# A hybrid attention and recurrence layer on one core: order around the last attention pair, and an engine for two copies

## The chip, the cores and the metric

The kernel runs on one core of one Trainium2 chip. The core has a matrix engine (TensorE, PE in the profile), VectorE (DVE), ScalarE (ACT), GpSimd (POOL), and queues that issue DMA transfers, of which SyncE's (SP) carries most. Each engine executes its own list of instructions in the order in which the program was built; engines wait for one another through semaphores. The metric is the device time of one execution in microseconds. Before the change three runs took 955.73 to 956.14 us, with a median of 955.91 us.

## The reference

One layer works on 1024 tokens of width 1024, with 16 learned tokens put in front (1040 columns in all):

```python
u = rmsnorm(h, g_pre_mix)
z = u @ w_in                      # -> q 512 | k 128 | v 128 | x_rec 512 | y_rec 512
attn = sliding_window_attention_with_sinks(q, k, v, sinks)   # window 128, 8 heads of 64, 2 kv heads
xr = causal_depthwise_conv(x_rec, conv_w, conv_b)            # 4 taps
hr = rg_lru(xr, w_a, b_a, w_x, b_x, lam)                     # two gates, then a linear scan over time
rec = gelu(y_rec) * hr
h = h + rmsnorm(concat(attn, rec) @ w_out, g_post_mix)
f = square(relu(rmsnorm(h, g_pre_ffn) @ w_ff1)) @ w_ff2      # 1024 -> 4096 -> 1024
out = h + rmsnorm(f, g_post_ffn)
```

Everything is float32. In the attention, each row of scores has its maximum taken (with the sink in it), then exp(s - m), the sum, the division, and the product with v.

## The kernel before, in words

Float32 accuracy is reached by splitting: every operand is held as a high part (rounded to the matrix engine's fast format, by a copy, L96 or L117) and a low part (the rest, by a subtraction on VectorE, L99 or L118). `mm3` (L123) makes a product of three matmuls: high with high (L125), high with low (L128), low with high (L129).

The work up to about 262 us is the mixing part, and it is what the change touches. After it come the output projection's rest and the feed-forward part, which take the remaining 690 us and which the diff does not touch.

The attention's eight query heads are treated as four pairs, j = 0 to 3. A pair is worked in two halves of 512 tokens, and a half in two steps bp of 256 tokens. `scores(j, half, q)` (L579) makes the score matmuls (L596, L600) into banks of PSUM with the tag "s", of which there are two; one bank holds one head's two blocks (i = 0, 1). VectorE takes each block's negated maximum (L616, one instruction that also writes the masked scores to SBUF and so empties that block), ScalarE the exponential (L624, seen as L82 in the profile, which is the line of the helper `lut`), GpSimd and VectorE sum and scale (L628 to L633). `attend(j, half, pairs)` (L637) transposes the result on the matrix engine (L644, banks "pt"), splits it (L96, L99), lets GpSimd cut the two sides of the window out of the two parts (L648, four of them in a step), and multiplies with v (L658: six matmuls in a step, banks "o"); ScalarE and VectorE then take the banks out (L671, L672).

Between the steps of the attention the kernel puts projections as fill for the matrix engine, one per half in the order q1, x1, q2, x2, q3, x3, y0, y1, then y2 and, behind the gates' code, y3. `project` (L257) runs each in pieces (two of 512 columns for q and y, four of 272 or 256 for x), with KC = 8 times `mm3` a piece, into banks "acc", of which there are two. Its `sink` takes the piece out of its bank:

- for q (L447), two 64-row halves, each a high part on ScalarE (L117) and then a low part on VectorE (L118);
- for x (L459), copies on ScalarE (L460);
- for y (L714), one copy on VectorE (L715). The y are the pieces that gate the recurrence.

A projection's weights are split when the one before it is begun (L96 and L99 into "ws", two pairs of buffers).

The recurrence is four chunks c. `gates(c)` (L789) multiplies the convolved x chunk with the gate weights (L800, into banks "s", "pt" and "o") and applies tanh; `decay`, `root`, `input_scale`, `input_gate`, `scan` and `rec_mult` follow, and with them the loads and splits of w_out (`load_wo`, L870; `split_wo`, L877). I call this the recurrent lane. Its VectorE order is written out by hand from L904 on with `queue`.

The order on each engine is made by a planner when the program is built: it takes, of the instructions that are ready by its own clock, the one with the smallest priority, which is the place in the program plus a delay of 1000 (FILL_LAG) for all of the fill but q1, q2 and q3 (`deferred`). Buffers of a tag go to whoever is planned to need one next. Three devices bend that order: `behind(name, ins)` (L106), which keeps `ins` behind the named instruction; `lut`, which chains all table functions on ScalarE; and `queue`. Two places use `behind` here: the low part of y0's weights stands behind the fourth maximum of pair 3 (L622), and the second piece of y1 is cut in two:

```python
if kc == 1 and begun is not None:            # L268, in project
    begun.append(ins)
if (c, t0) == (0, 696):                      # L806, in gates
    behind(ins.name, begun[1][1])
```

So `begun[1][1]` is the first matmul of kc = 1 in y1's second piece; it and what follows it in that piece stand behind the last gate matmul of chunk 0, and its three matmuls of kc = 0 may run ahead.

Of the kernel before, what the change touches and what calls it, by code (L numbers as in the profile page):

```python
# [18 lines left out]
KC = D // P  # L19
T = 1024  # L20
NMETA = 16
TT = T + NMETA
HD = 64
# [14 lines left out]
def hybrid_layer(  # L38
# [218 lines left out]
    def project(w, pieces, sink, begun=None):  # L257
        wh, wl = w
        for t0, n in pieces:
            acc = bank("acc")  # L260
            for kc in range(KC):
                uh, ul = u[kc]
                ins = mm3(
                    acc[:, :n], (wh[:, kc, :], wl[:, kc, :]),
                    (uh[:, t0 : t0 + n], ul[:, t0 : t0 + n]),
                    kc == 0, kc == KC - 1,
                )
                if kc == 1 and begun is not None:  # L268
                    begun.append(ins)
            sink(acc[:, :n], t0, n)  # L270

# [166 lines left out]
    def sink_v(acc, t0, n):  # L438
        if t0 == 0:
            nc.scalar.copy(vmt[:, META], acc[:, 0:NMETA])  # L440
        nc.scalar.copy(vt[:, t0 : t0 + n], acc)

    def new_q():

        q = pair("b", [P, T])

        def sink_q(acc, t0, n):  # L447
            c = slice(t0 - NMETA, t0 - NMETA + n)
            for h in range(2):
                r, o = HALF[h], HALF[1 - h]  # L450
                split_scaled(q[h][r, c], q[h][o, c], acc[r], HD ** -0.5)

        return q, sink_q

# [124 lines left out]
    def scores(j, half, q):  # L579

        g, pairs = j // 2, []
        for bp in range(2):
            sn = slot("c", [P, 4, 257])
            negm = small.tile([P, 4], F32, name="negm", tag="negm")
            den = small.tile([P, 4], F32, name="den", tag="den")
            rden = small.tile([P, 4], F32, name="rden", tag="rden")
            nc.vector.tensor_copy(
                sn.rearrange("p (h i) k -> p h i k", h=2)[:, :, :, 256],
                nsink[:, 2 * j : 2 * j + 2].to_broadcast([P, 2, 2]),
            )  # L590
            for h in range(2):
                sp_ = bank("s", (P, 2, 256))

                def qk(dst, b, hi, lo):
                    c = slice(b * P, (b + 1) * P)
                    nc.tensor.matmul(  # L596
                        dst, q[h][:, c], hi, start=True, stop=False,
                        skip_group_check=True,
                    )
                    nc.tensor.matmul(  # L600
                        dst, q[h][:, c], lo, start=False, stop=True,
                        skip_group_check=True,
                    )

                for i in range(2):
                    b = 4 * half + 2 * bp + i
                    if b == 0:
                        qk(sp_[:, i, 0:P], b, km[:, g, 0, :], km[:, g, 1, :])
                        qk(sp_[:, i, P:256], b, khh[g][:, 0:P], kl[g][:, 0:P])
                    else:  # L610
                        c = slice((b - 1) * P, (b + 1) * P)
                        qk(sp_[:, i, :], b, khh[g][:, c], kl[g][:, c])
                for i in range(2):
                    b = 4 * half + 2 * bp + i
                    k = 2 * h + i
                    top = nc.vector.tensor_tensor_reduce(  # L616
                        out=sn[:, k, 0:256], in0=sp_[:, i, :],
                        in1=mask1 if b == 0 else mask, scale=-1.0,
                        scalar=nsink[:, 2 * j + h : 2 * j + h + 1],
                        op0=ALU.add, op1=ALU.min, accum_out=negm[:, k : k + 1],  # L620
                    ).ins
                    if (j, half, bp, k) == (3, 0, 0, 3):  # L622
                        behind(top.name, *held_back)
                    lut(  # L624
                        sn[:, k, :], sn[:, k, :], AF.Exp, scale=-1.0,
                        bias=negm[:, k : k + 1], accum_out=den[:, k : k + 1],
                    )
            nc.vector.reciprocal(rden, den)  # L628


            one = sn[:, :, 0:P]
            nc.gpsimd.tensor_tensor(one, one, sn[:, :, P:256], op=ALU.add)
            nc.vector.tensor_tensor(one, one, rden.to_broadcast([P, 4, P]), op=ALU.mult)  # L633
            pairs.append(sn)
        return pairs

    def attend(j, half, pairs):  # L637
        g = j // 2
        o_ = slot("e", [P, 512])
        for bp, sn in enumerate(pairs):  # L640
            mh, ml = pair("c", [P, 4, 2, P])
            pt = bank("pt", (P, 4, P))
            for k in range(4):
                nc.tensor.transpose(pt[:, k, :], sn[:, k, 0:P], ident)  # L644
            split(mh[:, :, 1, :], ml[:, :, 1, :], pt)
            for m in (mh, ml):
                for side, op, sign in ((0, ALU.is_gt, 1), (1, ALU.is_ge, -1)):
                    nc.gpsimd.affine_select(  # L648
                        out=m[:, :, side, :], in_=f32(m)[:, :, 1, :],
                        pattern=[[0, 4], [-sign, P]], compare_op=op, fill=0.0,  # L650
                        base=0, channel_multiplier=sign,
                    )
            po = bank("o", (P, 2, 256))
            mhv, mlv = (m.rearrange("p (h i) s q -> p h (i s q)", h=2) for m in (mh, ml))

            def av(v, oc, n, pc, first, last):
                for k, m in enumerate((mhv, mlv)):
                    nc.tensor.matmul(  # L658
                        po[:, :, oc : oc + n], v, m[:, :, pc : pc + n],
                        start=first and k == 0, stop=last and k == 1,  # L660
                        skip_group_check=True,
                    )

            b = 4 * half + 2 * bp
            av(vk[g][:, b, :], 0, 256, P, True, False)
            av(vm[:, g, :] if b == 0 else vk[g][:, b - 1, :], 0, P, 0, False, False)
            av(vk[g][:, b + 1, :], P, P, 3 * P, False, True)
            c = slice(256 * bp, 256 * bp + 256)
            for h in range(2):
                r, o = HALF[h], HALF[1 - h]  # L670
                nc.scalar.copy(o_[r, c], po[o, h, :])  # L671
                nc.vector.tensor_tensor(o_[r, c], po[r, h, :], o_[r, c], op=ALU.add)  # L672
        ah, al = at[half][j // 2]
        split(ah[:, j % 2, :], al[:, j % 2, :], o_)
# [35 lines left out]
    def fill_y(c):  # L710
        def run(w):
            y = slot("b" if c == 1 else "d", [P, T])

            def sink(acc, t0, n):  # L714
                nc.vector.tensor_copy(y[:, t0 - NMETA : t0 - NMETA + n], acc)  # L715

            begun[c] = []
            project(w, REAL2, sink, begun[c])
# [70 lines left out]
    def gates(c):  # L789
# [3 lines left out]
        for t0, n in ((0, 348), (348, 348), (696, 344)):  # L793
# [10 lines left out]
                    if hold:  # L804
                        behind(hold, ins)
            if (c, t0) == (0, 696):  # L806
                behind(ins.name, begun[1][1])
            for s, t_ in enumerate((te, to)):
                shut[0] = lut(
                    t_[:, t0 : t0 + n], accs[s][:, :n], AF.Tanh, scale=0.5,  # L810
# [713 lines left out]
```

## Time and profile before

| | |
|---|---|
| median of three runs | 955.91 us (955.73 to 956.14) |
| the profiled execution | 955.25 us |
| its span, first to last instruction | 953.5 us |
| PE busy | 942.0 us, 99% of the span |
| DVE, ACT, POOL busy | 682.4, 498.3, 152.7 us |
| granted TensorE clock | 0.998 |

A row of a timeline has the start in us, the length in us, the engine, the line, the operation, the tiles written and read, the shape and the count of instructions merged into it; in brackets stands the idle time ahead of it and who ended it. A wait's row has the engine, tile and line that waited, the engine, tile and line that released it, and the total in us, the number of times and the longest. Matmuls overlap in the engine, so the distance from start to start is what one costs, not its length.

### The profile page before, as it was taken

The page shows a single profiled execution, that of the slowest core. Times are in us where ns is not written, and L with a number is a line of the kernel's source. Part 1 is how long each engine was busy: PE and PEld are TensorE (multiplying, and loading weights), DVE is VectorE, ACT ScalarE, POOL GpSimd, SP SyncE. Part 2 cuts the span into 40 slices and gives each one's busy share as a digit, 9 for nine tenths or more (in the row PEclk, how much of TensorE's full clock was granted, in tenths as well). Part 3 has the DMA queues.
Part 4 walks back from the last instruction along what each step waited for, and adds up shares of the span by engine and source line. Part 5 has one row for each costly group of instructions (what it writes and reads, how often), then busy time and mean ns, then how long its engine had stood idle before and what let it go on. Part 6 is the DMA issues. An engine that isn't in the chain of part 4 may idle for free.

```text
span 953.5 us, 12448 instructions
## 1 busy us (share of the span) xinstructions
PE 942.0 (99%) x4677; PEld 785.7 (82%) x4677; DVE 682.4 (72%) x968; ACT 498.3 (52%) x822; POOL 152.7 (16%) x196
## 2 busy tenths in 40 slices
PE   9999999999999999999999999999999999999997
PEld 8999998878788877888888878888888888888886
DVE  6679999777966886665755566567567676779884
ACT  7556676468355564443655565664433343445451
POOL 2115666500021100000111001100111100003020
PEclk9999999999999999999999999999999999999999
DMA  8121101203145457485646457644678865656422
GB/s 293 49 56 34 45 2 34 67 17 117 42 166 192 153 181 238 158 284 177 218 160 216 157 177 217 226 153 109 171 179 188 208 218 185 185 190 155 116 84 89
DMA packets 85629, 140.76 MB, mean 148 GB/s; under 512 B 5785, under 2 KB 48937, under 8 KB 85569
## 3 DMA queue, kind: packets, MB, share of 16 engines
q1 hardware_dynamic: 75104, 108.51, 36.1%
q0 software_dynamic: 9600, 29.36, 11.7%
q10 hardware_dynamic: 864, 2.10, 0.6%
q8 instruction: 37, 0.61, 0.3%
q14 instruction: 24, 0.19, 0.1%
HBM read 115.70 MB, written 23.07 MB: 146 GB/s over the span
## 4 chain that ended last, share of the span: by engine, by line
PE 88%; DVE 7%; ACT 2%; issue 1%; DMA 1%; POOL 1%; DVEq 0%; SPq 0%; ACTq 0%; POOLq 0%
PE ps_acc L125 10%; PE ps_acc L128 10%; PE ps_acc L129 10%; PE ps_pt L128 6%; PE ps_pt L129 6%; PE ps_pt L125 6%; PE ps_s L125 6%; PE ps_s L129 6%; PE ps_s L128 6%; PE ps_o L125 5%; PE ps_o L128 5%; PE ps_o L129 5%; DVE c L852 1%; PE ps_o L658 1%; PE ps_o L996 1%
## 5 line engine op out<-in xcount | busy, mean ns | idle before, releaser
L96 ACT CAST ws<-raw 128x1024 fp32r<-128x1024 f32 (+1 forms) x70 | 71.8, 1025 | 118.9 <-PE ps_o L128 45.8
L99 DVE TENSOR_TENSOR ws<-raw,ws 128x1024 fp32r<-128x1024 f32 (+1 forms) x71 | 85.4, 1203 | 45.5 <-ACT ws L96 45.5
L125 PE MATMUL ps_acc<-a,ws 128*128 128x256 f32 (+2 forms) x256 | 85.5, 334 | 1.1 <-ACT d L460 1.0
L129 PE MATMUL ps_acc<-a,ws 128*128 128x256 f32 (+2 forms) x256 | 85.0, 333 | 0.0
L128 PE MATMUL ps_acc<-a,ws 128*128 128x256 f32 (+2 forms) x256 | 85.0, 332 | 0.0
L99 DVE TENSOR_TENSOR b<-b,b 128x1024 fp32r<-128x1024 f32 (+2 forms) x48 | 57.6, 1199 | 25.5 <-PE ps_o L128 19.8
L96 ACT CAST ws<-e 128x1024 fp32r<-128x1024 f32 x42 | 44.0, 1047 | 57.0 <-PE ps_o L128 31.4
L96 ACT CAST b<-b 128x1024 fp32r<-128x1024 f32 (+2 forms) x48 | 49.5, 1030 | 38.8 <-DVE b L1022 36.4
L99 DVE TENSOR_TENSOR ws<-e,ws 128x1024 fp32r<-128x1024 f32 x42 | 51.3, 1222 | 20.0 <-ACT ws L96 20.0
L648 POOL TENSOR_SCALAR_AFFINE_SELECT c<-c 128x512 fp32r<-128x512 f32 x64 | 55.8, 893 | 26.8 <-ACT c L96 20.6
L125 PEld LDWEIGHTS ps_acc<-a,ws 128*128 128x128 f32 x256 | 48.2, 188 | 6.4 <-ACT d L460 1.2
L129 PEld LDWEIGHTS ps_acc<-a,ws 128*128 128x128 f32 x256 | 48.2, 188 | 5.1 <-issue 0.2
L178 POOL TENSOR_TENSOR rs<-ms,half_pow 128x1 f32<-128x1 f32 x26 | 19.3, 749 | 205.9 <-DVE ms L174 204.7
L128 PEld LDWEIGHTS ps_acc<-a,ws 128*128 128x128 f32 x256 | 48.1, 188 | 4.6 <-issue 0.4
L125 PE MATMUL ps_acc<-ws,b 128*128 128x512 f32 (+1 forms) x120 | 46.3, 385 | 0.0
L129 PE MATMUL ps_acc<-ws,b 128*128 128x512 f32 (+1 forms) x120 | 46.2, 385 | 0.0
L128 PE MATMUL ps_acc<-ws,b 128*128 128x512 f32 (+1 forms) x120 | 46.1, 384 | 0.0
L125 PE MATMUL ps_pt<-ws,b 128*128 128x512 f32 x112 | 44.2, 394 | 0.0
L128 PE MATMUL ps_pt<-ws,b 128*128 128x512 f32 x112 | 44.1, 393 | 0.0
L129 PE MATMUL ps_pt<-ws,b 128*128 128x512 f32 x112 | 43.9, 392 | 0.0
L125 PE MATMUL ps_s<-ws,b 128*128 128x512 f32 x110 | 43.4, 395 | 0.0
L129 PE MATMUL ps_s<-ws,b 128*128 128x512 f32 x110 | 43.2, 393 | 0.0
(429 smaller groups left out, 2720.9 us busy)
## 6 DMA issues: line engine op xcount, KB each, us to landing
raw<-in_w_ff_dram SPq DMA_DIRECT2D x58, 512.0 KB, 4.4
e<-in_w_ff_dram SPq DMA_DIRECT2D x42, 512.0 KB, 4.1
raw<-in_w_in_dram SPq DMA_DIRECT2D x12, 512.0 KB, 5.1
d<-in_w_ff_dram SPq DMA_DIRECT2D x12, 512.0 KB, 4.2
s_dram<-d POOLq DMA_DIRECT2D x12, 512.0 KB, 4.4
e<-in_w_ff_dram POOLq DMA_DIRECT2D x10, 512.0 KB, 5.8
raw<-in_w_ff_dram POOLq DMA_DIRECT2D x10, 512.0 KB, 5.8
c<-in_x_dram SPq DMA_DIRECT2D x8, 512.0 KB, 8.9
```

Of the source, the lines that this page charges most:

```text
L96: nc.scalar.copy(hi, src)
L99: low = nc.vector.tensor_tensor(lo, src, f32(hi), op=ALU.subtract).ins
L125: ins = nc.tensor.matmul(dst, lh, rh, start=start, stop=False, skip_group_check=True).ins
L128: nc.tensor.matmul(dst, lh, rl, start=False, stop=False, skip_group_check=True)
L129: last_mm[0] = nc.tensor.matmul(dst, ll, rh, start=False, stop=stop, skip_group_check=True).ins.name
L178: last_pow[0] = nc.gpsimd.tensor_tensor(rs[:n], ms[:n], half_pow[:n], op=ALU.pow).ins.name
L648: nc.gpsimd.affine_select(out=m[:, :, side, :], in_=f32(m)[:, :, 1, :], pattern=[[0, 4], [-sign, P]], compare_op=op, fill=0.0, base=0, cha ...
L658: nc.tensor.matmul(po[:, :, oc : oc + n], v, m[:, :, pc : pc + n], start=first and k == 0, stop=last and k == 1, skip_group_check=True,)
L852: return nc.vector.tensor_tensor_scan(r, a, gi, 0.0, op0=ALU.mult, op1=ALU.add).ins
L996: nc.tensor.transpose(pt[:, i, :], xn[:, kc * P : (kc + 1) * P], ident)
```

## The change

Four things are done.

1. `new_q`'s sink leaves the last pair of split instructions that it made in `q_made`. When `scores` makes pair 3's first block, that is the second half of q3's second piece. The first exponential of pair 3 is put behind that high part (on ScalarE) and the first maximum behind that low part (on VectorE).
2. The value products of the attention's very last step (j = 3, half = 1, bp = 1) are put behind `begun[1][2]`. `project` now lists the first matmul of every kc, so this is the matmul of kc = 2 in y1's first piece.
3. The two copies that take y0 out of its banks go from VectorE to ScalarE.
4. The cut in y1's second piece moves from kc = 1 to kc = 2 (`begun[1][KC + 2]` in the longer list).

```diff
@@ project
-                if kc == 1 and begun is not None:
+                if begun is not None:
                     begun.append(ins)
@@ new_q
+    q_made = []
+
...
-                split_scaled(q[h][r, c], q[h][o, c], acc[r], HD ** -0.5)
+                q_made[:] = split_scaled(q[h][r, c], q[h][o, c], acc[r], HD ** -0.5)
@@ scores
-                    lut(
+                    power = lut(
                         sn[:, k, :], sn[:, k, :], AF.Exp, scale=-1.0,
                         bias=negm[:, k : k + 1], accum_out=den[:, k : k + 1],
                     )
+                    if (j, half, bp, k) == (3, 0, 0, 0):
+                        behind(q_made[0].name, power)
+                        behind(q_made[1].name, top)
@@ attend, av
-                    nc.tensor.matmul(
+                    ins = nc.tensor.matmul(
                         po[:, :, oc : oc + n], v, m[:, :, pc : pc + n],
                         start=first and k == 0, stop=last and k == 1,
                         skip_group_check=True,
-                    )
+                    ).ins
+                    if (j, half, bp) == (NPAIR - 1, 1, 1):
+                        behind(begun[1][2].name, ins)
@@ fill_y
-                nc.vector.tensor_copy(y[:, t0 - NMETA : t0 - NMETA + n], acc)
+                copy = nc.scalar.copy if c == 0 else nc.vector.tensor_copy
+                copy(y[:, t0 - NMETA : t0 - NMETA + n], acc)
@@ gates
             if (c, t0) == (0, 696):
-                behind(ins.name, begun[1][1])
+                behind(ins.name, begun[1][KC + 2])
```

## The prediction

> **What bounds the kernel now.** I read the page's first part, then the waits of the matrix engine, then the busy time by stage, then PE's timeline at each wait, and last what VectorE, ScalarE and GpSimd did just ahead of it.
>
> ```profile
> span 953.5 us, 12448 instructions
> PE 942.0 (99%) x4677; PEld 785.7 (82%) x4677; DVE 682.4 (72%) x968; ACT 498.3 (52%) x822; POOL 152.7 (16%) x196
> ...
> PE ps_acc L125 <- ACT d L460: 1.0, 1, 1.0
> PE ps_o L658 <- POOL c L648: 0.9, 1, 0.9
> PE ps_acc L125 <- ACT a L1221: 0.7, 1, 0.7
> ...
> PE ps_acc L125 <- DVE b L715: 0.2, 1, 0.2
> ```
>
> PE is busy for 99% of the span, so what can be won without taking matmuls away is the time in which it waits. Apart from the start, the waits above are the large ones. Three of the four lie in the stages that the change touches; the one at L1221 is in the feed-forward part.
>
> ```profile
> 142.00:158.00 16.00, 15.05 (x100) 13.64 (x100) 15.68 (x35) 11.38 (x31) 9.84 (x9) 1.00 0.19 50
> 158.00:170.00 12.00, 12.00 (x101) 11.77 (x100) 8.18 (x27) 7.72 (x25) 8.83 (x11) 1.00 0.01 2
> 170.00:184.00 14.00, 13.44 (x66) 10.93 (x64) 13.84 (x17) 5.99 (x12) 8.99 (x9) 1.00 0.26 75
> 184.00:200.00 16.00, 15.46 (x78) 12.32 (x79) 8.24 (x12) 6.02 (x11) 0.29 (x1) 1.00 0.11 34
> 200.00:262.00 62.00, 61.94 (x294) 48.72 (x292) 55.14 (x54) 40.51 (x52) 0.00 (x0) 1.00 0.21 67
> ```
>
> The columns after the stage's length are PE, PEld, DVE, ACT and POOL busy, then the granted clock. VectorE is full in two stages (15.68 of 16 us, 13.84 of 14), and there PE loses time; between them it idles for 12 - 8.18 = 3.8 us. The three waits in PE's own order:
>
> ```profile
> 156.19 0.28 PE L600 MATMUL ps_s<-b,b 128*128 128x256 f32 x1
> 157.41 0.39 PE L125 MATMUL ps_acc<-a,ws 128*128 128x256 f32 x1 [0.95 <-ACT d L460]
> 157.64 0.28 PE L128 MATMUL ps_acc<-a,ws 128*128 128x256 f32 x1
> 157.76 0.28 PE L129 MATMUL ps_acc<-a,ws 128*128 128x256 f32 x1
> ...
> 182.11 1.33 PE L658 MATMUL ps_o<-c,b 128*128 128x512 f32 x7
> 184.35 0.98 PE L658 MATMUL ps_o<-c,b 128*128 128x512 f32 x5 [0.91 <-POOL c L648]
> 185.16 0.39 PE L125 MATMUL ps_acc<-a,ws 128*128 128x512 f32 x1
> 185.39 0.39 PE L128 MATMUL ps_acc<-a,ws 128*128 128x512 f32 x1
> ...
> 190.69 0.39 PE L125 MATMUL ps_acc<-a,ws 128*128 128x512 f32 x1
> 191.14 0.39 PE L129 MATMUL ps_acc<-a,ws 128*128 128x512 f32 x1
> 191.72 0.47 PE L125 MATMUL ps_acc<-a,ws 128*128 128x512 f32 x1 [0.19 <-DVE b L715]
> 192.03 0.39 PE L128 MATMUL ps_acc<-a,ws 128*128 128x512 f32 x1
> ```
>
> From start to start a matmul of 256 columns costs 157.76 - 157.64 = 0.12 us, one of 512 costs 185.39 - 185.16 = 0.23.
> First gap: the next start was due at 156.19 + 0.12, so 157.41 is 1.10 late, and the first matmul after it costs 0.23 in place of 0.12: 1.21 us.
> Second gap: of the seven value products three have 512 columns and four 256, so the eighth was due at 182.11 + 3 x 0.23 + 4 x 0.12 = 183.28; 184.35 is 1.07 late, and the five take 0.81 in place of 0.71: 1.17 us.
> Third gap: due at 191.14 + 0.23 = 191.37, so 0.35, and 0.31 in place of 0.23 after it: 0.43 us.
> Together 2.81 us.
>
> **Part 1, q3's second piece taken out first.** What held the first gap:
>
> ```profile
> 139.72 0.59 ACT L117 ACTIVATE b<-ps_acc 64x512 fp32r<-64x512 f32 x1 [2.17 <-PE ps_acc L129]
> 140.34 0.68 DVE L118 SCALAR_TENSOR_TENSOR b<-ps_acc,b 64x512 fp32r<-64x512 f32 x1 [0.52 <-ACT b L117]
> 141.09 0.59 ACT L117 ACTIVATE b<-ps_acc 64x512 fp32r<-64x512 f32 x1
> 141.72 0.69 DVE L118 SCALAR_TENSOR_TENSOR b<-ps_acc,b 64x512 fp32r<-64x512 f32 x1 [0.20 <-ACT b L117]
> 145.09 0.47 DVE L616 CUSTOM_DVE_ANT_0 c<-ps_s,mask,nsink 128x256 f32<-128x256 f32 x1
> ...
> 149.07 0.39 PE L129 MATMUL ps_acc<-a,ws 128*128 128x512 f32 x1
> 149.99 0.28 PE L596 MATMUL ps_s<-b,b 128*128 128x256 f32 x1
> ...
> 150.23 0.59 ACT L117 ACTIVATE b<-ps_acc 64x512 fp32r<-64x512 f32 x1
> ...
> 157.95 0.69 DVE L118 SCALAR_TENSOR_TENSOR b<-ps_acc,b 64x512 fp32r<-64x512 f32 x1
> ```
>
> The first four rows are q3's first piece: the two engines take turns on the bank, and four turns last 141.72 + 0.69 - 139.72 = 2.69 us. The second piece's matmuls end at 149.07 + 0.39 = 149.46, but its last turn ends at 157.95 + 0.69 = 158.64, because maxima and exponentials of pair 3 stand between the turns. Until then x3's second piece has one bank of "acc" alone, and has to wait for the copy of its own first piece (L460). With the turns first, the bank is free at 149.46 + 2.69 = 152.15 at the earliest, 4.1 us ahead of the 156.31 at which x3's second piece is due. The gap goes: -1.21.
>
> The price is that pair 3's first maximum moves from 145.09 to 152.15 or later, 7.1 us. Queued behind it on VectorE are its block's three other maxima, on ScalarE all exponentials (chained), and on PE the score matmuls of the next step (149.99), which need the bank "s" that the first two maxima empty. In the old order PE would stand from 149.99 until two maxima of 0.47 after 152.15 are through, 153.09: 3.1 us. In another order it has value products and x3's first piece to do, and the price is nothing. So part 1 lies between -1.21 and +1.9. I take -1.21, for the order is made anew with the hold in it, and this stretch of PE has work of both kinds. VectorE does the same work in another order, and the 3.8 idle us behind 158 take up what is late.
>
> By the Trainium skill ("PSUM — Partial Sum Buffer", section "PSUM bank collisions raise a hardware error") only accesses of two engines to the same bank and the same quadrant of 32 partitions must be kept apart, and the two halves of q lie in different quadrants. By that the second ScalarE turn could run beside the first VectorE turn, and the bank would be free one turn of 0.7 us sooner; the rows above show strict turns, and I go by them. The sum is the same by both.
>
> **Parts 2 and 3, the last value products and y0's copies.**
>
> ```profile
> 178.22 0.37 ACT L671 COPY e<-ps_o 64x256 f32<-64x256 f32 x1 [2.26 <-DVE e L672]
> 178.61 0.59 ACT L96 CAST c<-ps_pt 128x512 fp32r<-128x512 f32 x1
> ...
> 181.04 3.26 POOL L648 TENSOR_SCALAR_AFFINE_SELECT c<-c 128x512 fp32r<-128x512 f32 x3 [0.81 <-DVE c L99]
> ...
> 183.83 1.29 DVE L715 COPY d<-ps_acc 128x512 f32<-128x512 f32 x2
> ```
>
> GpSimd's last selection ends at 181.04 + 3.26 = 184.30, and the value products wait for it. The change puts seven matmuls of y1 (kc = 0, 1 and the first of 2) in front: 7 x 0.23 = 1.61 us of work against a gap of 1.17: -1.17, with 0.44 to spare. They need a bank that y0 has left at about 183. On VectorE the two copies run at 183.83 to 185.12, too late; ScalarE has 2.26 idle us at 175.96, after y0's first piece, and a copy there costs as much as the 0.59 of the cast from "pt" of the same 128x512. So the copies cost ScalarE 2 x 0.59 and PE nothing, and relieve VectorE of 1.29 us. If they wait behind something on ScalarE, part 2 falls back to its old wait.
>
> **Part 4, the cut at kc = 2.** y1's second piece may run six matmuls ahead of the gates in place of three, 6 x 0.23 = 1.38 us. The third gap is y2's wait for the bank of y1's first piece:
>
> ```profile
> 190.88 0.69 DVE L715 COPY b<-ps_acc 128x512 f32<-128x512 f32 x1 [1.73 <-PE ps_acc L129]
> ```
>
> That bank is usable at 191.72, 191.72 - 190.69 = 1.03 us after the first piece's end, less than the 1.38. The gap goes: -0.43. Gate matmuls of chunk 0 come three matmuls (0.69 us) later against y1, those of chunk 1 do not, since y1's rest behind chunk 0 is shorter by the same three.
>
> **Is what PE wins kept?** At the end of the recurrent lane VectorE and PE meet:
>
> ```profile
> 260.65 1.22 DVE L99 TENSOR_TENSOR a<-raw,a 128x1024 fp32r<-128x1024 f32 x1
> ...
> 261.47 0.39 PE L125 MATMUL ps_pt<-a,b 128*128 128x512 f32 x1
> 261.92 0.50 PE L128 MATMUL ps_pt<-a,b 128*128 128x512 f32 x1
> ```
>
> The matmul at 261.92 was due at 261.70 and starts when the low part of w_out's last chunk ends, at 261.87. So the lane has no slack, and PE's gain counts only as far as the lane moves with it. The lane starts from the gates of chunk 0 and 1, which PE reaches in its own order; VectorE is busy for only 8.24 of 16 us ahead of it (184 to 200). So it moves with PE, and I take the whole sum.
>
> Sum: -1.21 - 1.17 - 0.43 = -2.81 against the profiled execution's 955.25 us: 952.4. The median of the runs lies 0.66 above it, so 953.1 for the median, 0.29% less. A measurement of this kernel can tell about 0.2% (1.9 us) from no change.
>
> **The rivals.**
> *The wait only moves (same).* PE waits for the "s" banks about as long as it did for "acc" (1.21, inside the 0 to 3.1 above); the other two gaps go: 955.9 - 1.6 = 954.3. For it: VectorE is full from 142 to 158. Against: banks "s" had the same owner and no wait before.
> *The lane does not move (same).* PE arrives 2.8 earlier at 261.92 and waits there: 955.9, less the 0.4 of the matmuls around it: 955.5. For it: no slack. Against: VectorE's idle time ahead of the lane.
> *Pair 3 is late through to the gates (slower).* The 7.1 us go down VectorE's queue; the 3.8 idle us and the 1.29 of y0's copies take up a part, and 7.1 - 3.8 - 1.3 = 2.0 reach the gates (which need the banks "s", "pt" and "o" of the last step) and the lane: 957.9. It decides from 1.9 us of lateness at the gates. For it: the lane has no slack. Against: the fourth maximum of the same block moves far less than the first, and the sum over the block waits for the fourth anyway.
> *The copies stand in ScalarE's way (same or slower).* ScalarE works in order. If y0's second copy stands ahead of the cast at 178.61, that cast waits for y0's matmuls until about 182.3 and the copy's 0.59, 4.3 us; the value products come 4.3 later, less 1.6 of cover: 2.7 later, less 1.21 and 0.43: 955.9 + 1.1 = 957.0, or 958.2 if the first gap stays. Against: the 2.26 idle us lie ahead of that cast, and a piece that is not ready is planned later. By the Trainium skill (the same page, section "Engine vs sequencer instructions") the queue of ScalarE is strictly first in, first out; the trace agrees, in that the 2.26 us above are a wait with later work queued behind it.
>
> **How the numbers follow.** All three gaps close: 0.52, its own range 952.1 (L1221's 0.7 and the 0.2 at 261.92 gone as well) to 954.0 (two thirds of the sum). The wait only moves: 0.15. The lane does not move: 0.06. Pair 3 late: 0.20. Copies in the way: 0.07, half of it slower. So faster 0.52, same 0.15 + 0.06 + 0.03 = 0.24, slower 0.24. The range goes from 951.7 (952.1 less the 0.4 between the highest and lowest run) to 958.2, the last rival's upper price; I leave 0.05 below and 0.13 above.
>
> **What the changed profile would show.** Part 1: both turns of q3's second piece done by about 153, no wait of PE on L460, the first maximum at 152 or later; wrong if PE waits on L616 or "s" instead. Part 2: seven matmuls of y1 between the two sets of value products and no wait on L648. Part 3: L715 twice on ScalarE before 183. Part 4: six matmuls of y1's second piece ahead of y2. The sum: w_out's last low part 2 to 3 us earlier than 260.65. The prediction is wrong if the gates come later, or if VectorE has longer idle time in the lane.

## The result, and the profile after

The changed kernel takes 954.62 us (median of 22 runs, 953.52 to 955.56); the kernel before, run beside it, 955.99. The ratio is 0.9982 with a 95% interval of 0.9977 to 0.9988: 1.7 us less by the ratio (the medians lie 1.4 apart). That is clear of no change, and just under the 1.9 us that was called measurable. Run again in the experiments it gave 0.998 (0.997 to 0.9989). The forecast was 953.1 us, 2.81 us less. The profiled execution took 953.78 us, its span 952.1 against 953.5.

The page's first part for the changed kernel:

```profile
span 952.1 us, 12450 instructions
...
PE 940.5 (99%) x4677; PEld 785.3 (82%) x4677; DVE 681.8 (72%) x966; ACT 499.4 (52%) x824; POOL 154.5 (16%) x196
```

The waits of its matrix engine (its lines are numbered 2 higher from `new_q` on, 5 higher in `attend` and 8 higher from y's `sink` on, so L653 is the old L648):

```profile
PE ps_o L663 <- POOL c L653: 1.2, 3, 0.5
PE ps_acc L125 <- ACT a L1229: 0.7, 1, 0.7
```

The waits on L460 and L715 are gone. The wait on GpSimd's selections has not gone; it is 1.2 us in three pieces where it was 0.9 in one: 0.5 and 0.5 in the stages here, and 0.2 ahead of 140 us. The busy time by stage, in the columns of before:

```profile
142.00:158.00 16.00, 15.49 (x104) 14.02 (x103) 15.57 (x31) 9.08 (x23) 9.14 (x8) 1.00 0.19 50
...
170.00:184.00 14.00, 13.51 (x70) 11.12 (x69) 13.19 (x16) 5.89 (x13) 11.08 (x11) 1.00 0.27 76
184.00:200.00 16.00, 16.00 (x81) 12.56 (x80) 8.33 (x11) 7.68 (x16) 0.64 (x1) 1.00 0.10 34
200.00:262.00 62.00, 62.00 (x299) 49.70 (x298) 58.62 (x60) 43.45 (x58) 0.00 (x0) 1.00 0.24 78
```

PE still idles 0.5 us in the first stage and 0.5 in the third, and no longer in the fourth. The places, on PE's timeline:

```profile
149.97 1.33 PE L663 MATMUL ps_o<-c,b 128*128 128x512 f32 x7
151.81 0.97 PE L663 MATMUL ps_o<-c,b 128*128 128x512 f32 x5 [0.51 <-POOL c L653]
...
155.95 0.29 PE L129 MATMUL ps_acc<-a,ws 128*128 128x272 f32 x1
156.07 0.28 PE L125 MATMUL ps_acc<-a,ws 128*128 128x256 f32 x1
...
182.48 0.97 PE L663 MATMUL ps_o<-c,b 128*128 128x512 f32 x5 [0.49 <-POOL c L653]
...
184.89 0.39 PE L663 MATMUL ps_o<-c,b 128*128 128x512 f32 x1
...
186.04 0.86 PE L663 MATMUL ps_o<-c,b 128*128 128x512 f32 x5
```

The first gap is closed: x3's second piece follows its first after 0.12 us (156.07). So are the value products of the last step (184.89 and 186.04, no wait). But the products of pair 2's last step now wait at 151.81, and those of the last step but one at 182.48.

Waits alone miss a part of the loss, so the table counts all of it. For each stage it adds up how much later each matmul started after the one in front than at its own pace (0.23 us for 512 columns, 0.12 for 256, 0.125 for 272, 0.08 for the gates' 344 and 348, the usual distances on the timeline). The stages are counted from the same early matmul (the 900th), since the start varies from execution to execution. "Lead" is how much earlier than in the kernel before PE's last matmul starts, counted in the same way; "tail" is the time from the issue of the last output transfer to the end of the span.

| kernel | 142–162 | 162–190 | 190–232 | 232–275 | lead | tail |
|---|---|---|---|---|---|---|
| before | 2.01 | 1.76 | 3.29 | 0.52 | – | 3.03 |
| after | 1.29 | 1.54 | 2.12 | 0.16 | 2.41 | 3.99 |

PE has won 7.58 - 5.11 = 2.47 us, near the forecast of 2.81 but in other places: 0.7 where 1.2 was expected, 0.2 in place of 1.2, 1.2 in place of 0.4, and 0.4 at 262. And a microsecond of it is lost again behind the last matmul.

### The profile page after: what moved, and what is told of

It reads as the page before. It is cut to its first block, busy times and chain, and to the rows that moved or that the text cites. A ratio compares the mean times of both kernels' runs of the same rounds, so it can differ in the third digit from the quotient of the medians.

```text
span 952.1 us, 12450 instructions
## 1 busy us (share of the span) xinstructions
PE 940.5 (99%) x4677; PEld 785.3 (82%) x4677; DVE 681.8 (72%) x966; ACT 499.4 (52%) x824; POOL 154.5 (16%) x196
## 4 chain that ended last, share of the span: by engine, by line
PE 94%; DVE 2%; POOL 2%; ACT 1%; issue 0%; DMA 0%; DVEq 0%; ACTq 0%; POOLq 0%
PE ps_acc L125 11%; PE ps_acc L128 11%; PE ps_acc L129 11%; PE ps_pt L125 7%; PE ps_pt L129 7%; PE ps_pt L128 6%; PE ps_s L125 6%; PE ps_s L129 6%; PE ps_s L128 6%; PE ps_o L128 5%; PE ps_o L125 5%; PE ps_o L129 5%; POOL c L653 1%; PE ps_o L663 1%; PE ps_o L1004 1%; PE ps_s L602 1%
## 5 line engine op out<-in xcount | busy, mean ns | idle before, releaser
L99 DVE TENSOR_TENSOR ws<-raw,ws 128x1024 fp32r<-128x1024 f32 (+1 forms) x71 | 85.6, 1205 | 42.8 <-ACT ws L96 42.6
L99 DVE TENSOR_TENSOR b<-b,b 128x1024 fp32r<-128x1024 f32 (+2 forms) x48 | 57.5, 1198 | 23.2 <-PE ps_o L128 18.0
L99 DVE TENSOR_TENSOR ws<-e,ws 128x1024 fp32r<-128x1024 f32 x42 | 51.3, 1222 | 20.2 <-ACT ws L96 20.2
L653 POOL TENSOR_SCALAR_AFFINE_SELECT c<-c 128x512 fp32r<-128x512 f32 x64 | 56.2, 902 | 24.0 <-ACT c L96 20.3
```

The costliest lines, as they stand in the source:

```text
L99: low = nc.vector.tensor_tensor(lo, src, f32(hi), op=ALU.subtract).ins
L653: nc.gpsimd.affine_select(out=m[:, :, side, :], in_=f32(m)[:, :, 1, :], pattern=[[0, 4], [-sign, P]], compare_op=op, fill=0.0, base=0, cha ...
```

## The experiments

My theories: (H), from the comparison, the hold of part 1 pays back what it wins, because the selections behind it come late; (L), which I came to only after e4, the cut of part 4 is the change's main part, because it decides in how many pieces the gate matmuls run and in which order the recurrent lane stands; and the rest of the gain is lost in the last transfer. The rival is the prediction's own account: each part is worth its gap.

| kernel | median us | ratio to before | 142–162 | 162–190 | 190–232 | 232–275 | lead | tail |
|---|---|---|---|---|---|---|---|---|
| e1, without part 1 | 953.16 | 0.9971 (0.9958 to 0.9983) | 2.00 | 1.06 | 1.64 | 0.15 | 2.44 | 3.23 |
| e2, part 1 alone | 956.69 | 1.0009 (1.0 to 1.0018) | 1.29 | 2.81 | 3.29 | 0.60 | -0.61 | 3.05 |
| e3, without part 3 | 952.84 | 0.9971 (0.9959 to 0.9983) | 1.29 | 1.53 | 1.70 | 0.15 | 2.76 | 3.01 |
| e4, without part 4 | 959.36 | 1.0039 (1.0024 to 1.0055) | 1.29 | 1.52 | 2.89 | 3.58 | -2.28 | 3.24 |
| e5, after again | 954.20 | 0.998 (0.997 to 0.9989) | 1.28 | 1.54 | 2.12 | 0.15 | 2.58 | 3.98 |
| e6, part 4 alone | 953.94 | 0.9977 (0.9967 to 0.9987) | 2.01 | 1.81 | 1.92 | 0.16 | 1.75 | 3.03 |
| e7, hold a step later | 952.76 | 0.9962 (0.9949 to 0.9974) | 1.72 | 0.95 | 1.64 | 0.15 | 2.79 | 3.24 |
| e8, e1 with y1's end behind gates | 955.84 | 0.9993 (0.9984 to 1.0003) | 2.01 | 1.09 | 3.69 | 0.41 | 0.11 | 3.23 |
| e9, ScalarE code moved | 955.85 | 1.0 (0.9992 to 1.0009) | 1.30 | 1.51 | 2.12 | 0.15 | 1.21 | 3.96 |
| e10, e7 without part 3 | 953.75 | 0.9979 (0.997 to 0.9988) | 1.69 | 1.55 | 1.93 | 0.16 | 1.98 | 3.15 |
| e11, without part 2 | 954.20 | 0.9984 (0.9975 to 0.9993) | 1.28 | 1.56 | 2.13 | 0.16 | 2.31 | 3.97 |
| e12, SyncE code moved | 955.40 | 0.9993 (0.9984 to 1.0002) | 1.29 | 1.58 | 2.09 | 0.16 | 1.14 | 3.86 |

**Part 1 taken out (e1), and alone (e2).**

```diff
-                    if (j, half, bp, k) == (3, 0, 0, 0):
-                        behind(q_made[0].name, power)
-                        behind(q_made[1].name, top)
```

> The changed kernel without part 1 (no hold on pair 3's first maximum and exponential); parts 2 to 4 stay. Theory H (the hold pays back what it wins: it closes the 1.2 us gap on L460 but makes the softmax of pair 3 late, so that value products wait for GpSimd's selections, 0.78 us at 151 and 0.76 at 182 in the changed kernel) expects the L460 gap of 1.2 back, no wait on GpSimd, and the last output transfer issued within 0.5 us of the changed kernel's 948.09; time 954.6, give or take 0.5. Rival F (the forecast: the hold is worth its 1.2 us) expects that issue at 949.3 and 955.8 us.

> Part 1 alone in the kernel before. Theory H expects nothing won: the L460 gap closed (-1.2), a wait of 0.8 on GpSimd at 151, and at the last value products a wait of about 2 us in place of 1.2, since GpSimd's last selection ends at about 184.6 as in the changed kernel: last output issued at 950.5 to 951.1 (950.52 before), 955.9 to 956.5 us. Rival F expects the issue at 949.3 and 954.7 us.

Without the hold gap 1 is back and the wait at 151.81 is gone, together 0.71 more in the first stage. In the second stage the wait at 182.48 is gone, and a smaller one, for y0's copy on ScalarE, is there in its place (0.48 less together; 0.2 of that, and of the 0.71, is one group of transposes that falls in the first stage here and in the second there):

```profile
PE ps_acc L125 <- ACT d L720: 0.2, 1, 0.2
```

In the third it is 0.48 less because the gates run in four groups, and with the hold in five (what a group costs follows at e8). The stages add up to 4.85 against 5.11, so the hold costs PE 0.26 us; its final lead is about the same, 2.44 against 2.41 and 2.58. The time, 953.16, lies below what theory H expected (954.1 at the least), mostly because the last transfer was short (tail 3.23 against 3.99). Alone, the hold made nothing faster. The waits of the matrix engine with the hold alone, and the two of them in 162–190:

```profile
PE ps_o L663 <- POOL c L653: 2.0, 3, 1.0
```

```profile
182.67 1.20 PE L663 MATMUL ps_o<-c,b 128*128 128x512 f32 x6 [0.47 <-POOL c L653]
184.88 0.97 PE L663 MATMUL ps_o<-c,b 128*128 128x512 f32 x5 [1.01 <-POOL c L653]
```

So 162–190, where e2 changes nothing by hand, loses 1.05 us more than before, while the first stage wins 0.72. Gap 2 itself grew little (1.01 of idle time in place of 0.91). About 0.7, with the restart, is a new wait at the products of the step before the last, and 0.2 the transposes that change stage. This is theory H. How the lateness gets there is seen in the timelines of the changed kernel's ScalarE, VectorE and GpSimd:

```profile
150.21 0.58 ACT L117 ACTIVATE b<-ps_acc 64x512 fp32r<-64x512 f32 x1
...
154.06 0.59 ACT L117 ACTIVATE b<-ps_acc 64x512 fp32r<-64x512 f32 x1 [0.87 <-DVE b L118]
```

```profile
145.07 1.21 DVE L99 TENSOR_TENSOR ws<-raw,ws 128x1024 fp32r<-128x1024 f32 x1
...
151.28 0.48 DVE L618 CUSTOM_DVE_ANT_0 c<-ps_s,mask,nsink 128x256 f32<-128x256 f32 x1
...
152.09 1.22 DVE L99 TENSOR_TENSOR ws<-raw,ws 128x1024 fp32r<-128x1024 f32 x1
153.34 0.68 DVE L118 SCALAR_TENSOR_TENSOR b<-ps_acc,b 64x512 fp32r<-64x512 f32 x1
154.83 0.69 DVE L118 SCALAR_TENSOR_TENSOR b<-ps_acc,b 64x512 fp32r<-64x512 f32 x1
155.56 0.48 DVE L618 CUSTOM_DVE_ANT_0 c<-ps_s,mask,nsink 128x256 f32<-128x256 f32 x1
```

```profile
143.25 8.51 POOL L653 TENSOR_SCALAR_AFFINE_SELECT c<-c 128x512 fp32r<-128x512 f32 x7 [0.26 <-DVE c L99]
...
178.09 6.56 POOL L653 TENSOR_SCALAR_AFFINE_SELECT c<-c 128x512 fp32r<-128x512 f32 x7 [0.56 <-DVE c L99]
```

and in those of GpSimd, VectorE and PE before:

```profile
143.26 7.72 POOL L648 TENSOR_SCALAR_AFFINE_SELECT c<-c 128x512 fp32r<-128x512 f32 x7 [0.26 <-DVE c L99]
```

```profile
145.89 1.21 DVE L99 TENSOR_TENSOR ws<-raw,ws 128x1024 fp32r<-128x1024 f32 x1
```

```profile
150.46 2.02 PE L658 MATMUL ps_o<-c,b 128*128 128x512 f32 x12
```

Three things follow. First, the turns on the bank. The first turn on ScalarE is done at 150.79, but its partner on VectorE starts only at 153.34: two maxima of the same step, which the hold does not name, and a low part of 1.22 us stand in front. So the held maximum runs at 155.56, 10.5 us later than before and not 7.1. The turns were strict again: ScalarE's second waited 0.87 us for VectorE's first, done at 154.02. By the Trainium skill ("PSUM — Partial Sum Buffer", section "PSUM bank collisions raise a hardware error") halves in different quadrants need not be kept apart; the trace has the turns all the same, and no run here shows what enforces them.

Second, GpSimd. The same seven selections take 8.51 us in place of 7.72 and end at 151.76 in place of 150.98. Taken one by one, a selection lasts 0.64 us, but 3.0 to 3.2 or 1.6 where VectorE works on two operands in SBUF (L99 on weights, L694). Without the two maxima in front, VectorE begins that work at 145.07 and not at 145.89, so three selections get through ahead of it and not four. By the Trainium skill ("SBUF — State Buffer", section "SBUF: two separate sides") GpSimd and a VectorE operation with two SBUF inputs take turns on a shared port; the trace agrees, with these lengths.

Third, PE. The four score matmuls of pair 3's next step stood ahead of pair 2's last value products; with the bank "s" held they move behind them, so the products start at 149.97 and not at 150.46. The eighth is due at 149.97 + 1.17 = 151.14, half a microsecond earlier, and meets selections that come 0.8 later. With the end of before, 150.98, it would not have waited. Later the selections of pair 3's last two steps run as one chain from 178.09 to 184.65, and the products of the first of them wait at 182.48.

**The hold one step later (e7), and the same with the copies on VectorE (e10).**

```diff
-                    if (j, half, bp, k) == (3, 0, 0, 0):
+                    if (j, half, bp, k) == (3, 0, 1, 0):
```

> The changed kernel with the hold of part 1 moved one step later: the first exponential and maximum of pair 3's second step (bp = 1) in place of those of the first step stand behind the second half of q3's second piece. Theory H (the hold of the changed kernel costs as much as it wins, because the first maximum went to 155.56 us and GpSimd's selections behind it came late): here the first step's maxima stay at about 145, the wait of the matrix engine on L460 or L462 is gone, no wait on the selections (L653) at 151.81 is there and the one near 182.5 is shorter or gone; time 0.8 to 1.5 us below the changed kernel and 0 to 1 us below the changed kernel without part 1 (ratio to the kernel before 0.9962 to 0.9972). Rival theory Q (any hold in that stretch pushes something): the second step's maxima are held to about 153, its selections are late and the matrix engine waits there 1 us or more; time as the changed kernel or slower, ratio 0.9975 or more.

```profile
PE ps_pt L649 <- DVE c L638: 0.5, 1, 0.5
```

This is the only wait on PE between 136 and 300 us. The first step's maxima stand at 145.01 and 145.41 again, the seven selections end at 150.91, the next scores are back in front of the products; gap 1 is closed, and 0.5 us is lost at a transpose instead. It has the lowest time of all, 0.9962 against 0.998 for the changed kernel on the same chip, and PE's largest lead, 2.79 against 2.44 without any hold (the intervals of e7, e1 and e3 overlap). Much of the difference in time to the changed kernel is the short last transfer (tail 3.24 against 3.98). By the stages PE loses 4.46, against 5.11 with the hold where it was and 4.85 without any: held one step later, part 1 wins 0.4 us of its 1.2. So what was wrong with part 1 was mainly the block it held.

> The kernel with the hold one step later (its ratio was 0.9962), and y0's copies back on VectorE: parts 2 and 4, and part 1 at the second step. Theory V (VectorE has room for the two copies here too, as it had in the changed kernel, where leaving them on VectorE cost nothing): no new wait, the matrix engine within 0.2 us of the kernel with the copies on ScalarE, ratio 0.9955 to 0.997. Rival theory W (with the hold later, VectorE is full to about 184 us and the two copies of 0.65 us come late): y1's first bank is late and the matrix engine waits for L723 by 0.5 to 1.3 us, ratio 0.997 to 0.998.

```profile
PE ps_acc L125 <- DVE d L723: 0.6, 1, 0.6
...
PE ps_pt L649 <- DVE c L638: 0.5, 1, 0.5
```

Here part 3 does what the prediction said of it: with the copies on VectorE, y1's bank is late and PE waits 0.6 us (0.95 becomes 1.55 in 162–190).

**Part 3 taken out (e3), part 2 taken out (e11).**

```diff
-                copy = nc.scalar.copy if c == 0 else nc.vector.tensor_copy
+                copy = nc.vector.tensor_copy
```

> The changed kernel with y0's two copies back on VectorE. Theory: the copies are what frees the bank for the seven matmuls of y1 that stand in front of the value products; PE then waits for L715 at about 182.5 for 1 to 2 us, and the last output is issued 1 to 2 us later than 948.09; 955.6 to 956.6 us. Rival: since GpSimd makes PE wait there anyway (0.76 us), the copies come in that shadow, and the issue stays within 0.5 us of 948.09; 954.6 us.

```diff
-                    if (j, half, bp) == (NPAIR - 1, 1, 1):
-                        behind(begun[1][2].name, ins)
```

> The changed kernel without part 2: the last value products are not put behind y1's third matmul. With the hold of part 1 in place the order made without part 2 has ten matmuls of y1 between the first and the second of these products by itself. Theory H (with GpSimd's selections as late as the hold makes them, part 2 has nothing left to do): the waits of the changed kernel (two on GpSimd's selections, near 151.8 and 182.5) and nothing else, the matrix engine within 0.2 us of the changed kernel in its lead over the kernel before, ratio 0.9971 to 0.9985, by whether the last transfer is held up. Rival theory P (part 2 is worth its gap, as predicted): a wait on the selections of the last step of 0.9 to 1.1 us is back and the time is 1.2 us above the changed kernel, ratio 0.999 or more.

With the hold in place, neither is needed; the wait of 1 to 2 us that I expected in e3 did not come. Without part 3 PE is even 0.2 to 0.35 us further ahead (the first gates run as one group of 18 and not as 6 and 12), and the tail is 3.01. Without part 2 the planner puts eleven matmuls of y1 among the last products by itself, and stages, lead and time are those of the changed kernel. Without the hold part 2 does win its gap: parts 2, 3 and 4 together (e1) lose 1.06 in 162–190, part 4 alone (e6) 1.81.

**Part 4 taken out (e4), and alone (e6).**

```diff
-                behind(ins.name, begun[1][KC + 2])
+                behind(ins.name, begun[1][KC + 1])
```

> The changed kernel with the cut of y1's second piece back at kc = 1. Theory C (part 4 closes the 0.43 us gap and also lets the gate matmuls stand together: five interruptions of the projections by gates in the changed kernel, six before, each costing PE about 0.55 us) expects six interruptions again and the gap back: last output issued 0.6 to 1.2 us after 948.09; 955.2 to 955.8 us. Rival F (part 4 is the gap alone) expects 0.43 us: 948.5 and 955.0 us.

> The kernel before with part 4 alone: the cut in y1's second piece at kc = 2, nothing else. Theory L (the cut decides the order of the gates and of the recurrent lane): y1's last matmuls all stand ahead of the gates of chunk 1, its weight buffers come free earlier, y3's weights are split at about 202 to 205 us in place of 208 to 211, the gates stand in four whole groups of 18, w_out's last low part is 3 to 4 us earlier than 260.65, and the waits at L715 and at 261.92 are gone; the waits at L460 (1.0) and L648 (0.9) stay. The matrix engine wins 0.43 + 0.33 + one interruption less (0.55) = 1.3 us: about 1.3 us below the kernel before, ratio 0.9986. Rival theory G (the cut is worth its gap alone, as predicted): 0.43 us, ratio 0.9995, w_out's last low part at about 260.2.

Both theories of e4 were far off: it is not 0.4 to 1.2 us slower than the changed kernel but about 5.5 by the ratios (1.0039 against 0.998 to 0.9982) and 4.7 in PE's lead (its seven runs spread from 957.88 to 963.58, and the profiled one is the lowest). And part 4 alone gives 0.9977, as much as all four parts; in PE's lead it is 1.75 against 2.41, and the last transfer makes up the difference (tail 3.03 against 3.99). The term was forecast at 0.43. Where it acts is seen in e4's waits of PE and VectorE's timeline:

```profile
PE ps_pt L128 <- DVE a L99: 2.9, 2, 1.8
```

```profile
228.72 1.24 DVE L850 SCALAR_TENSOR_TENSOR c<-b,c 128x1040 f32<-128x1040 f32 x1 [4.46 <-ACT c L82]
...
238.69 1.23 DVE L99 TENSOR_TENSOR a<-raw,a 128x1024 fp32r<-128x1024 f32 x1 [5.84 <-ACT a L96]
...
264.88 1.22 DVE L99 TENSOR_TENSOR a<-raw,a 128x1024 fp32r<-128x1024 f32 x1
```

The lane has become the limit: VectorE idles 10.3 us in two pieces, and w_out's last low part starts at 264.88. In the changed kernel, and with part 4 alone, it starts at

```profile
204.71 1.21 DVE L99 TENSOR_TENSOR ws<-raw,ws 128x1024 fp32r<-128x1024 f32 x1
...
256.45 1.22 DVE L99 TENSOR_TENSOR a<-raw,a 128x1024 fp32r<-128x1024 f32 x1
```

```profile
205.59 1.21 DVE L99 TENSOR_TENSOR ws<-raw,ws 128x1024 fp32r<-128x1024 f32 x1
...
257.69 1.22 DVE L99 TENSOR_TENSOR a<-raw,a 128x1024 fp32r<-128x1024 f32 x1
```

The upper row of each is the low part of y3's weights (210.93 before, 209.83 in e4). It can run when y1 no longer needs its pair of weight buffers. With the cut at kc = 1 the last two matmuls of y1 stand behind the gates of chunk 1; with the cut at kc = 2 all stand ahead of them. So ScalarE's cast of y3's weights, which fills these buffers, goes ahead of the table functions of chunk 1 in the changed kernel (first row) and stands behind most of them before (second row):

```profile
201.59 1.05 ACT L96 CAST ws<-raw 128x1024 fp32r<-128x1024 f32 x1 [1.03 <-PE ps_acc L128]
```

```profile
208.19 1.07 ACT L96 CAST ws<-raw 128x1024 fp32r<-128x1024 f32 x1
```

The cast, then the low part of y3's weights, then the next load of w_out (205.94 in place of 212.19) all come about 6 us sooner.

**y1's end put behind the gates (e8).** To see whether that is the cause, I took the kernel of e1, left the cut at kc = 2, and put only y1's last three matmuls behind the gates of chunk 1:

```diff
                 behind(ins.name, begun[1][KC + 2])
+            if (c, t0) == (1, 696):
+                behind(ins.name, begun[1][2 * KC - 1])
```

> The changed kernel without part 1, and with y1's last three matmuls (kc = 7 of its second piece) put behind the last gate matmul of chunk 1. The cut stays at kc = 2. Theory L (with the cut at kc = 1 time was lost because y1's last matmuls slipped behind the gates of chunk 1, which freed its weight buffers late): y3's weights are split at about 207 to 210 us in place of 202 to 205, w_out's loads and casts come later, VectorE idles 4 us or more twice between 225 and 245, the matrix engine waits about 2 us on VectorE's low part (L99) near 262, and the time is 3 to 5 us above the changed kernel without part 1 (956 to 958 us, ratio 1.000 to 1.003). Rival theory C (what cost time with the cut at kc = 1 was the lone position of the cut, y2's wait for its bank): nothing but one more interruption of a projection, 0.55 us: 953.7 us, ratio 0.9977.

The lane falls back to its old place: y3's weights at 211.68, w_out's last low part at 261.85, of which 1.58 is a later start of this whole execution. The time rises by about 2.1 us by the ratios (0.9971 to 0.9993), less than theory L's 3 to 5 and more than its rival's 0.55. So the order part of theory L is shown. But PE does not wait at 262, and 2.05 of the 2.3 us that it loses against e1 lie in 190–232. There the gates run in seven groups (three of them of three matmuls), in e1 and e6 in four, in the changed kernel in five, before in six. One group whole, with part 4 alone:

```profile
208.83 0.40 PE L128 MATMUL ps_acc<-a,ws 128*128 128x512 f32 x1
209.16 0.42 PE L803 MATMUL ps_s<-b,b 64*128 64x348 f32 x1
209.16 0.42 PE L803 MATMUL ps_pt<-b,b 64*128 64x348 f32 x1
209.42 0.32 PE L803 MATMUL ps_s<-b,b 64*128 64x348 f32 x1
...
210.52 0.32 PE L803 MATMUL ps_pt<-b,b 64*128 64x344 f32 x1
210.79 0.50 PE L125 MATMUL ps_acc<-a,ws 128*128 128x512 f32 x1
211.14 0.39 PE L128 MATMUL ps_acc<-a,ws 128*128 128x512 f32 x1
```

and one of the small ones in e8:

```profile
210.64 0.39 PE L125 MATMUL ps_acc<-a,ws 128*128 128x512 f32 x1
210.95 0.73 PE L805 MATMUL ps_o<-b,b 64*128 64x344 f32 x3
211.61 0.50 PE L128 MATMUL ps_acc<-a,ws 128*128 128x512 f32 x1
211.95 0.40 PE L129 MATMUL ps_acc<-a,ws 128*128 128x512 f32 x1
```

Gate matmuls of 64 rows start in pairs, a pair every (210.52 - 209.42) / 7 = 0.157 us. From 208.83 to 211.14 are 2.31 us; two projection matmuls (0.46) and nine pairs (1.41) explain 1.87, so going into the group and out of it costs 0.44. In e8's group of three, 1.31 less 0.46 less three halves of 0.157 leaves 0.61, for the three have no partners. These costs stand in no list of waits. They rebuild the third stage of the table: four groups make 4 x 0.44 = 1.76 (1.64 in e1), the changed kernel's five 2.20 (2.12), and e8's four groups and three of three matmuls 3.59 (3.69); the kernel before, with five, one of three and gap 3 of 0.43, comes to 3.24 (3.29).

One thing stays open: e8 brings back the lane of the kernel before, not that of e4, which stands 4.2 us later still (264.88 against 260.65) with the same cut as before. Which of parts 1 to 3 does that was not tested.

**The last transfer (e5, e9, e12).**

> The changed kernel once more, unaltered. Its matrix engine ends 2.4 us earlier than in the kernel before, and its last output transfer was issued 2.43 us earlier (948.09 against 950.52), but in its profile that transfer landed 3.04 us after its issue, in the kernel before 2.08. Theory T (the long landing was of that one execution): the last transfer lands after about 2.1 us, the span is about 951.1 us, and the median lies 2.4 us below the kernel before, ratio 0.9975. Theory R (the long landing belongs to this kernel): 3.0 us again, a span of about 952.1, and a median 1.4 to 1.7 us below, ratio 0.9982 to 0.9985.

The long tail is back in e5 (3.98), so it belongs to the kernel. The changed kernel's DMA view from 947 us on has the landing, and its view from 949.6 to 950.4 what moved then:

```profile
out_dram<-a ACTq DMA_DIRECT2D x1, 256.0 KB, 3.0
```

```profile
q10 hardware_dynamic: 27, 0.02, 11.1%
q14 instruction: 1, 0.01, 2.4%
```

The last transfer, on ScalarE's queue, lands after 3.0 us (2.1 before), and a packet of an instruction queue falls in amid its last packets. In all five profiles with a tail of 3.9 to 4.0 (after, e5, e9, e11, e12) that packet starts 1.5 to 1.7 us behind the last issue, and the longest packet of the transfer takes 0.23 to 0.29 us; in the nine with 3.0 to 3.2 it starts elsewhere, and the longest takes 0.09. I tried to push it away with eight tiny copies on ScalarE, then with eight tiny loads in SyncE's queue:

```diff
     lut(root, half_pow, AF.Sqrt, scale=-1.0)
+    for _ in range(8):
+        nc.scalar.copy(spare, eps_t)
...
+    for i in range(8):
+        behind(last_wo[0], nc.sync.dma_start(spare[:, i : i + 1], x[0:1, i : i + 1]).ins)
```

> The changed kernel with eight tiny copies (one column each) added on ScalarE at the start of the program, where it waits for the first loads; the order on TensorE and VectorE is the same as in the changed kernel. It asks why the last output transfer of the changed kernel landed 3.0 us after its issue in both of its profiles (issue 948.09 and 948.17), in the kernel before and in the seven other kernels 2.0 to 2.1. In both of its profiles a packet of 8 KB of the instruction queue starts 1.66 us after that issue, amid the last packets of the transfer; in the others it starts 0.4 to 0.5 us ahead of the issue or 3.5 to 3.9 us behind it. Theory F (that packet holds up the transfer): if the added instructions shift it away from there, the transfer lands after about 2.1 us again and the time is about 0.9 us below the changed kernel: 953.2 us, ratio 0.997. If it starts at the same place again, 3.0 us and 954.2. Rival theory N (the landing is long for another reason, such as what the transfers ahead of it do, which are the same here): 3.0 us wherever the packet starts, and ratio 0.998.

> The changed kernel with eight tiny loads (one number each) added in SyncE's queue behind w_out's last load, about 240 us, where SyncE has little to do; the order on TensorE, VectorE and ScalarE is that of the changed kernel. Eight instructions added on ScalarE left the packet of the instruction queue where it was, 1.64 us behind the last output's issue, and the landing at 3.0 us. Theory S (the packet carries SyncE's instructions, and its place follows their count; where it starts amid the last transfer, that lands 0.9 us later): the packet starts eight of SyncE's instructions earlier, ahead of the last issue, the last transfer lands after about 2.1 us, the span is about 951.2 and the time about 0.9 us below the changed kernel: 953.2 us, ratio 0.997. Rival theory N: the packet starts at about 1.65 us again and the landing is 3.0, or it moves and the landing is 3.0 all the same; 954.2 us, ratio 0.998.

Neither moved it (1.64 and 1.52 us behind the issue; tails 3.96 and 3.86), and both runs lost time elsewhere: PE's lead in their profiles sank to 1.2 and 1.1, with the four stages as in the changed kernel. So that the packet delays the transfer is likely from fourteen profiles but not shown, and which engine's instructions it carries stays open.

## Why the prediction was right or wrong

- **What bounds the kernel, and the direction: right.** Time was won by closing PE's waits in the attention, and PE's 2.47 us are near the forecast 2.81. That is partly luck: two terms were too large and one too small.
- **Part 1 (-1.21 taken, bounds -1.21 to +1.9): right on its gap, wrong on the price.** The step that failed is "in another order it has value products and x3's first piece to do, and the price is nothing". The value products themselves then waited for GpSimd, whose selections the sum did not ask about: 0.5 us at 151.81 and 0.5 at 182.48, each about 0.8 with the restart behind it. The gates also ran in one group more, 0.48 us, which the sum did not ask about either. In the end the hold moved PE's lead by nothing (e1) or by -0.61 (e2). "152.15 at the earliest" became 155.52 for the bank, since two maxima and a low part of 1.22 us kept VectorE from its turn.
- **Part 2 (-1.17): right without the hold** (e1 against e6: 0.75 in its stage; no wait on GpSimd in e1, but 0.2 us of waiting for y0's copy, with the restart behind it), idle with it (e11). The forecast "no wait on L648" held for the last step and failed for the one before it.
- **Part 3 (nothing on PE, 1.29 us off VectorE): right that ScalarE has room.** The copies ran at 181.96 and 183.92, behind the cast of 178.18 and not ahead of it, so that rival fell. But they did not use the idle time at 175.96, and the second missed the "before 183"; without the hold the first came only at 183.24, and PE waited for it (e1), so "PE nothing" is not quite right. That part 2 needs them held only in the better order (e10: 0.6 us), not in this one (e3).
- **Part 4 (-0.43): the term that was mis-sized.** The gap did close. But the cut decided in how many groups the gates run (six before, five in the changed kernel, four with part 4 alone) and when y1 frees its weight buffers: 1.37 us in 190–232 and 0.36 behind it with part 4 alone (e6). The prediction counted the moved matmuls only against the wait, not what the planner would do around them.
- **"So it moves with PE": right, and more.** The last low part came 4.2 us earlier (256.45), not 2 to 3, and PE's wait at 261.92 went. Without part 4 the lane limits PE by 2.9 us (e4), so "the lane has no slack" was the sentence to follow further.
- **The sum: its conversion into time failed by a microsecond.** Nothing in the sum looks behind the last matmul. The last issue is 2.43 us earlier, the end of the span 1.4.
- **The rivals.** "The wait only moves" came nearest, at 954.3 against 954.62 and 954.20, by another road: PE waited at the value products for GpSimd, not at the "s" banks. "Pair 3 is late through to the gates" did not happen; with the lane that was found, the gates came earlier.

## What to carry to other kernels

When an instruction is held back, ask also what moves forward into its place: here VectorE's work on SBUF came 0.8 us earlier and shut GpSimd out, and the price of the hold was paid in products of another pair; holding the next step instead kept 0.4 us of the 1.2. Where a planner makes the order, count how often each edit makes the matrix engine change between kinds of matmul, and which buffers come free when; for part 4 both together moved more time than the wait that the edit was meant for. And follow a gain to the end of the span: what the matrix engine wins can be lost in the last transfer.

## What was not expected of the hardware

- Going from matmuls of 128 rows to those of 64 and back costs 0.44 us a group, and two of 64 rows start together (209.16 twice). By the Trainium skill ("TensorEngine Tiling (Array Packing)", section "Key Properties") changing the mode drains the engine and tiles work in parallel; the trace agrees, with these numbers.
- One selection on GpSimd took 0.64 us, 1.6 or 3.2, by what VectorE did beside it.
- The landing of the same 256 KB went from 2.1 to 3.0 us in four of fourteen profiles, and a fifth (e12), for which no landing is recorded, has the same long tail. Each time an instruction packet of 8 KB stands among its last packets.
- The time to the 900th matmul was 1.6 to 1.9 us longer than usual in the profiles of e8, e9 and e12, and within 0.5 us in all others; e8 changes nothing there. It was not looked into.
